# Keys and values by tokens in an mLSTM encoder: square blocks turned on VectorE and placed by four stores, instead of transposes on TensorE

## The chip, the cores and the metric

The kernel runs on one core of one Trainium2 chip. A core has TensorE (matrix products, "PE" in the profile, its weight loads "PEld"), VectorE ("DVE"), ScalarE ("ACT"), GpSimd ("POOL"), SyncE ("SP", which here only issues DMAs) and 16 DMA engines. The metric is device time in microseconds (us), the median of several runs.

## The reference, cut to what matters

One layer of a bidirectional encoder on 1280 tokens (1024 of a prompt, 256 of a sample) with 1024 channels. A normalised, modulated input `h` goes through one wide product `p = h @ w_in`; its columns are split into a convolution branch, gates, and the query, key and value of a matrix memory with 4 heads of 256 channels, worked out in chunks of 128 tokens and in both directions:

```python
h = rms_norm(x, norm_g) * (1.0 + scale) + shift
p = h @ w_in
cb, cc, cx, cz, q, k, v, o, mz, gpre, gmerge = split_combined(p)
...
# for each chunk of 128 tokens, qc, kc, vc: (batch, head, 128 tokens, 256 channels)
S = jnp.einsum('bhtd,bhsd->bhts', qc, kc) * Dexp
num = jnp.einsum('bhts,bhsd->bhtd', S, vc) + inter_w[..., None] * jnp.einsum('bhtd,bhde->bhte', qc, C)
...
C_new = decay[..., None, None] * C + jnp.einsum('bhs,bhsd,bhse->bhde', w, kc, vc)
```

The sum over `d` in the first line wants keys with channels on the partitions; the sums over tokens `s` in the second and the last want keys and values with tokens on the partitions. All of it is float32.

## The kernel before

The kernel has three stages. The first, which the change touches, makes all columns of `p`; the second (`Sweep`, `Pairs`) runs the matrix memory, with the convolution branch's projection as filler on TensorE; the third merges, projects and normalises.

**The products of the first stage.** Everything there lies with channels on the partitions and tokens along the free axis. Columns of `w_in` are taken in pairs of 128, tokens in two halves of 640 (`TH2`), the 1024 input channels in two halves: a 2 x 2 block product, done with seven products instead of eight (class `Strassen`). Each product is a job (function `go`): 24 pairs of a weight load and a matmul over 320 tokens (line 755), since each operand is split into a high and a low part and three of the four part products are taken. The weights of a job are prepared some steps ahead: DMA (line 318) into one of 3 `raw` tiles, sums of blocks on VectorE (`comb`, line 628), the high part on ScalarE (`wh`, line 329), the low part on GpSimd (`wl`, line 330). The result of a job stands in one of 3 PSUM tiles `acc`; VectorE adds it to an earlier part result (`plus`, line 672) into a tile `q` of 128 x 640, of which there are 5 (`new_q`, a ring used in the order of creation).

**The pairs of the heads.** For each of the 4 heads there is a pair for the keys, one for the values and one for the queries (`head_pairs`), those of head 0 about a sixth of the way into the span, those of heads 1 to 3 at the end of the first stage. Four of the seven jobs of a pair finish a result: 128 channels x 640 tokens, in jobs 2, 5, 6 and 7. A result of keys or queries is stored as it is (`kT_dr`, `qT_dr`, line 321). A result of keys or values goes through `by_tokens`, which turns it so that tokens are on the partitions, and stores it into `kn_dr` or `v_dr` (tokens x channels in DRAM), whence the second stage loads it. There are 4 heads x 2 x 4 = 32 such turns.

**One turn before.** TensorE transposes the five 128 x 128 blocks of the result (line 885) into two PSUM tiles `misc`, three and two blocks; ScalarE copies them (line 888) into a tile `q` called `vt`; one DMA stores `vt` with runs of 128 channels, 512 B each, 640 of them.

**The order.** Operations are recorded, not issued: `op(engine, cost, function, r=reads, w=writes)`. At the end of the first stage `board.play()` simulates all engines with the costs as written, and issues each engine's operations in the order in which that simulation began them. Each engine then works its list strictly in order, waiting on semaphores. A DMA is an operation of SP: 0.4 us to issue, then its size over a rate of 375 KB per us, then 2.2 us to land. In that simulation a turn of TensorE is given 1.0 us of slack (`slack=1.0`), so that it is put behind matmuls of the next job. While TensorE waits for the operand of one instruction, all that stands behind it in its list waits too; the same holds for VectorE and for SP.

`thirds`, which is also in the stretch of heads 1 to 3, makes part of the modulation on VectorE (line 1174) with two small matmuls (line 1181) at the end, also into `misc`. After the last pair, the first loads of the second stage are already in SP's list (`first_y`, into tiles `b00`, `b10`).

Of the kernel before, what the change touches and what calls it, by code (L numbers as in the profile page):

```python
# [16 lines left out]
P = 128  # L17
# [12 lines left out]
TH2 = T // 2  # L30
# [10 lines left out]
class Board:  # L41
# [25 lines left out]
    def buf(self, pool, shape, dt, tag, bufs, t=None):  # L67
        b = self.Buf(pool, shape, dt, tag, bufs, t)
        self.places.setdefault((id(pool), tag), []).append(b)
        return b  # L70

    def op(self, eng, us, f, r=(), w=(), after=(), low=False, slack=0.0):

        o = self.Op()
        o.eng, o.us, o.f, o.low, o.step, o.n, o.played, o.slack = eng, us, f, low, self.step, len(self.ops), False, slack
        o.before = set(after)
        for t in r:
            if t in self.writer:
                o.before.add(self.writer[t])
        for t in w:  # L80
            o.before.update(self.readers.get(t, ()))
            if t in self.writer:
                o.before.add(self.writer[t])
        for t in w:
            self.writer[t], self.readers[t] = o, []
        for t in r:
            if t not in w:
                self.readers.setdefault(t, []).append(o)
        o.before.discard(o)
        o.bufs = list(dict.fromkeys(b for t in (*r, *w) for b in (t if isinstance(t, tuple) else (t,)) if isinstance(b, self.Buf)))  # L90
        for b in o.bufs:
            b.users.append(o)
        self.ops.append(o)
        return o
# [87 lines left out]
def encoder_kernel(  # L182
# [7 lines left out]
    V, A, G, PE = nc.vector, nc.scalar, nc.gpsimd, nc.tensor  # L190
# [35 lines left out]
    ident = const.tile([P, P], F32, name="ident")  # L226
# [70 lines left out]
    op, buf = board.op, board.buf  # L297
# [22 lines left out]
    def store(kb, dst, src, r, w=()):  # L320
        op("SP", kb, lambda: dma(dst, src()), r=r, w=w)
# [236 lines left out]
    def qtile():  # L558
        return buf(rp, [P, TH2], F32, "q", 5)
# [5 lines left out]
    def misc_buf():  # L565
        return buf(psA, [P, 512], F32, "misc", 2)
# [19 lines left out]
    def whole(b):  # L586
        return Slice(b, slice(0, TH2))

    def new_q():
        return whole(qtile())  # L590
# [285 lines left out]


    def by_tokens(dst, t, r0, l):
        vt = new_q()
        for j0, jn in ((0, 3), (3, 2)):  # L880
            pv = misc_buf()

            def turn(j0=j0, jn=jn, pv=pv):
                for j in range(jn):
                    PE.transpose(pv[:, j * P:(j + 1) * P], t()[:, (j0 + j) * P:(j0 + j + 1) * P], ident[:])  # L885

            op("PE", .12 * jn, turn, r=[t.tok], w=[pv], slack=1.0)
            op("ACT", .2 + .1 * jn, lambda j0=j0, jn=jn, pv=pv: A.copy(vt()[:, j0 * P:(j0 + jn) * P], pv[:, :jn * P]),
               r=[pv], w=[(vt.b, j0)])
        store(320, dst[l * TH2:(l + 1) * TH2, r0:r0 + P].rearrange("(c p) d -> p c d", p=P),  # L890
              lambda: vt().rearrange("p (c d) -> p c d", d=P), [(vt.b, 0), (vt.b, 3)])

    def head_pair(col, dst, h):
        def result(b, l):
            r0 = h * HD + b * P

            def f(t):
                if col != CQ:
                    by_tokens(kn_dr if col == CK else v_dr, t, r0, l)
                if dst is not None:  # L900
                    store(320, dst[r0:r0 + P, l * TH2:(l + 1) * TH2], t, [t.tok])
            return None, f

        return Strassen(col + h * HD, col + h * HD + P, result(0, 0), result(1, 0), result(0, 1), result(1, 1))
# [716 lines left out]
    def second(s):  # L1621
        h, i = divmod(s - 10, 10)
        return (h, two_[h].order[i], i) if 0 <= h < NH else (None, None, None)
# [3 lines left out]
    for s in range(10 * NH + 15):  # L1627
# [4 lines left out]
        h, c, i = second(s - 3)  # L1632
        if h is not None and h + 2 < NH and c in (5, 7, 9):
            load_head(h + 2, (5, 7, 9).index(c))
        h, i = divmod(s, 10)
        mark = len(board.ops)
        if h < NH:
            c, d = one[h].order[i], one[h].d
# [8 lines left out]
        h, c, i = second(s)  # L1647
# [9 lines left out]
        h, c, i = second(s - 2)  # L1657
        if h is not None:
            prs[h, c - c % 2].values(c)
        h, c, i = second(s - 4)  # L1660
# [185 lines left out]
```

## Time and profile before

| | |
|---|---|
| median of 3 runs | 1730.31 us (1727.86 to 1730.43) |
| the profiled execution, its own time | 1726.71 us |
| span of the profiled execution | 1724.6 us |
| mean granted TensorE clock | 0.992 |
| busy: PE, PEld, DVE, ACT, POOL | 97%, 92%, 57%, 35%, 39% |
| chain that ended last: PE, DVE, issue | 91%, 5%, 2% |

The span runs from the first instruction to the last; the execution's own time is 2.1 us longer. Busy matmuls are pipelined, so a busy TensorE is not one at its peak; the time that a group of matmuls costs is read from the chain or from the starts of its neighbours. Where several engines are busy at once, only the one that the others wait for sets the time; the chain of waits tells which it was, and the table by stretches how much room the others have.

### The profile page before, as it was taken

The page shows a single profiled execution, that of the slowest core. Times are in us where ns is not written, and L with a number is a line of the kernel's source. Part 1 is how long each engine was busy: PE and PEld are TensorE (multiplying, and loading weights), DVE is VectorE, ACT ScalarE, POOL GpSimd, SP SyncE. Part 2 cuts the span into 40 slices and gives each one's busy share as a digit, 9 for nine tenths or more (in the row PEclk, how much of TensorE's full clock was granted, in tenths as well). Part 3 has the DMA queues.
Part 4 walks back from the last instruction along what each step waited for, and adds up shares of the span by engine and source line. Part 5 has one row for each costly group of instructions (what it writes and reads, how often), then busy time and mean ns, then how long its engine had stood idle before and what let it go on. Part 6 is the DMA issues. An engine that isn't in the chain of part 4 may idle for free.

```text
span 1724.6 us, 27940 instructions
## 1 busy us (share of the span) xinstructions
PE 1676.9 (97%) x10702; PEld 1591.3 (92%) x10702; DVE 974.6 (57%) x1657; ACT 604.4 (35%) x1185; POOL 679.5 (39%) x499
## 2 busy tenths in 40 slices
PE   7889999999999999999999999999999999999997
PEld 1789999899999999999999899999888889998986
DVE  1795433456555565566666765642247777565645
ACT  2753333224554222222222222222256565333322
POOL 1124333235665566667766533333210101323412
PEclk9899999999999999999999999999999999999999
DMA  9234323224553222222222434336878865684631
GB/s 332 87 109 146 115 91 121 64 74 122 148 155 108 57 68 68 80 80 63 65 61 89 141 108 138 117 117 231 284 232 273 269 199 162 219 282 135 229 112 61
DMA packets 217562, 241.88 MB, mean 140 GB/s; under 512 B 12645, under 2 KB 174677, under 8 KB 217429
## 3 DMA queue, kind: packets, MB, share of 16 engines
q1 hardware_dynamic: 217248, 240.06, 43.5%
q8 instruction: 85, 1.39, 0.3%
q14 instruction: 49, 0.39, 0.1%
q10 hardware_dynamic: 180, 0.04, 0.0%
HBM read 171.16 MB, written 68.89 MB: 139 GB/s over the span
## 4 chain that ended last, share of the span: by engine, by line
PE 91%; DVE 5%; issue 2%; ACT 1%; DMA 1%; ACTq 0%; SPq 0%; POOL 0%; DVEq 0%; POOLq 0%
PE acc L755 59%; PE u L1365 3%; PE qc L1347 3%; PE accd L1520 2%; PE accd L1521 2%; PE accd L1522 2%; PE accd L1733 2%; PE accd L1734 2%; PE accd L1732 2%; PE acc L1587 2%; PE acc L1588 2%; PE acc L1589 2%; PE acc L480 2%; PE misc L885 1%; PE misc L1408 1%
## 5 line engine op out<-in xcount | busy, mean ns | idle before, releaser
L672 DVE TENSOR_TENSOR q<-acc,q 128x640 f32<-128x640 f32 x272 | 220.6, 820 | 259.9 <-PE acc L755 249.5
L330 POOL TENSOR_TENSOR wl<-comb,wh 128x512 fp32r<-128x512 f32 x176 | 247.2, 1405 | 304.2 <-ACT wh L329 293.2
L330 POOL TENSOR_TENSOR wl<-raw,wh 128x512 fp32r<-128x512 f32 x136 | 191.6, 1409 | 250.9 <-ACT wh L329 245.1
L755 PE MATMUL acc<-xt,wh 128*128 128x320 f32 x1408 | 264.4, 310 | 0.0
L755 PEld LDWEIGHTS acc<-xt,wh 128*128 128x128 f32 x1408 | 220.6, 188 | 0.1
L329 ACT CAST wh<-comb 128x512 fp32r<-128x512 f32 x176 | 108.9, 619 | 243.6 <-PE acc L755 236.1
L329 ACT CAST wh<-raw 128x512 fp32r<-128x512 f32 x136 | 84.4, 621 | 286.5 <-PE acc L755 203.3
L755 PE MATMUL acc<-xt,wl 128*128 128x320 f32 x704 | 160.4, 309 | 0.0
L1548 POOL TENSOR_TENSOR wl<-raw,wh 128x512 fp32r<-128x512 f32 x28 | 36.3, 1300 | 233.7 <-ACT wh L1547 233.7
L755 PEld LDWEIGHTS acc<-xt,wl 128*128 128x128 f32 x704 | 117.7, 188 | 0.0
L628 DVE TENSOR_TENSOR comb<-raw 128x512 f32<-128x512 f32 x88 | 76.7, 872 | 46.7 <-DMA raw<-in_w_in_dram 31.2
L822 POOL TENSOR_TENSOR big<-big,q 128x640 f32<-128x640 f32 x48 | 78.8, 1641 | 37.1 <-DVE q L672 28.8
L572 ACT ACTIVATE q<-q,zero 128x640 f32<-128x640 f32 x76 | 63.2, 831 | 80.4 <-DVE q L672 74.8
L628 DVE TENSOR_TENSOR comb<-raw,comb 128x512 f32<-128x512 f32 x44 | 44.2, 1004 | 78.5 <-POOL wl L330 78.5
L755 PE MATMUL acc<-b00H,wh 128*128 128x320 f32 x352 | 83.0, 316 | 0.0
L755 PE MATMUL acc<-t2L,wh 128*128 128x320 f32 x352 | 80.3, 310 | 2.1 <-DVE t2L L384 2.1
L755 PE MATMUL acc<-b11H,wh 128*128 128x320 f32 x352 | 80.9, 310 | 1.5 <-ACT wh L329 1.5
L755 PE MATMUL acc<-t3H,wh 128*128 128x320 f32 x352 | 81.6, 313 | 0.0
L1520 PE MATMUL accd<-y,wh 128*128 128x320 f32 x256 | 79.9, 313 | 1.5 <-DVE og L1498 1.5
L755 PE MATMUL acc<-t2H,wh 128*128 128x320 f32 x352 | 80.8, 311 | 0.4 <-ACT t2H L383 0.4
L755 PE MATMUL acc<-b10H,wh 128*128 128x320 f32 x352 | 80.6, 309 | 0.4 <-DVE q L672 0.4
L755 PE MATMUL acc<-b11H,wl 128*128 128x320 f32 x352 | 80.1, 308 | 0.9 <-POOL wl L330 0.9
(320 smaller groups left out, 4195.4 us busy)
## 6 DMA issues: line engine op xcount, KB each, us to landing
raw<-in_w_in_dram SPq DMA_DIRECT2D x96, 256.0 KB
raw<-in_w_in_dram SPq DMA_DIRECT2D x46, 512.0 KB
th<-th_dr SPq DMA_DIRECT2D x32, 320.0 KB
th_dr<-q SPq DMA_DIRECT2D x28, 320.0 KB
raw<-in_w_proj_conv_dram SPq DMA_DIRECT2D x16, 512.0 KB
k<-kn_dr SPq DMA_DIRECT2D x64, 128.0 KB
raw<-in_w_proj_mlstm_dram SPq DMA_DIRECT2D x16, 512.0 KB
raw<-in_w_out_dram SPq DMA_DIRECT2D x16, 512.0 KB
```

Source lines behind the costliest of these rows:

```text
L329: op("ACT", .63, lambda: A.copy(wh[:], src()), r=r, w=[wh])
L330: op("POOL", 1.4, lambda: G.tensor_tensor(out=wl[:], in0=src(), in1=fp(wh[:]), op=ALU.subtract), r=[*r, wh], w=[wl])
L480: op("PE", .88, lambda h=h, j=j, kt=kt, wa=wa: PE.matmul(pada[h][0:4, j, :], cz4()[:, kt, :], wa()[:, j * 512:(j + 1) * 512], start=kt == ...
L572: A.activation(out, in_, AF.Tanh, bias=zero[:, 0:1], scale=0.5)
L628: op("DVE", .9, lambda: V.tensor_tensor(out=t[:], in0=x(), in1=y(), op=o), r=[x.tok, y.tok], w=[t])
L672: op("DVE", .82, lambda: V.tensor_tensor(out=two(dst()), in0=acc[:, :, 0:TQ], in1=two(t()), op=ALU.add), r=[acc, t.tok], w=[dst.tok])
L755: PE.matmul(acc[:, q, 0:TQ], st_[:, k_, :], m_[:, q * TQ:(q + 1) * TQ], start=k_ == 0 and n == 0, stop=k_ == 3 and n == 2)
L822: op("POOL", 1.65, lambda: G.tensor_tensor(out=dst(), in0=dst(), in1=t(), op=ALU.mult), r=[dst.tok, t.tok], w=[dst.tok])
L1347: PE.matmul(pq[:, 0:HD + 2], qTs[i][:, kd, c * P:(c + 1) * P], C[:, kd, :], start=kd == 0, stop=kd == 1)
L1365: PE.matmul(pu[:, db, 0:HD + 2], k[:, db * P:(db + 1) * P], wv[:], start=True, stop=True)
L1520: PE.matmul(accs[q][:, :TQ], wh, yH, start=kt == 0, stop=False)
L1548: op("POOL", 1.36, lambda wh=wh, wl=wl, src=src: G.tensor_tensor(out=wl[:], in0=src(), in1=fp(wh[:]), op=ALU.subtract), r=[raw, wh], w=[wl])
```

## The change

In `by_tokens` the transposes on TensorE, the two PSUM tiles and the copies on ScalarE are gone. One VectorE instruction turns the whole 128 x 640 tile in square blocks of 32 x 32, each in its place: `vt[32a+i, 32b+j] = t[32a+j, 32b+i]`. Now partition 32a+i holds, for each block b of 32 tokens, 32 channels of token 32b+i. The exchange of the blocks' places is left to the stores: for each of the four groups a of 32 partitions, one DMA of 80 KB writes runs of 32 channels (128 B), 32 x 20 = 640 of them, into the channel columns r0+32a to r0+32a+31 of the tokens. The bytes stored are the same 320 KB; the runs are a quarter as long and four times as many, and SP issues four DMAs where it issued one. In the simulation that makes the order, VectorE's turn costs 0.85 us.

```diff
     def by_tokens(dst, t, r0, l):
+
         vt = new_q()
-        for j0, jn in ((0, 3), (3, 2)):
-            pv = misc_buf()
-
-            def turn(j0=j0, jn=jn, pv=pv):
-                for j in range(jn):
-                    PE.transpose(pv[:, j * P:(j + 1) * P], t()[:, (j0 + j) * P:(j0 + j + 1) * P], ident[:])
-
-            op("PE", .12 * jn, turn, r=[t.tok], w=[pv], slack=1.0)
-            op("ACT", .2 + .1 * jn, lambda j0=j0, jn=jn, pv=pv: A.copy(vt()[:, j0 * P:(j0 + jn) * P], pv[:, :jn * P]),
-               r=[pv], w=[(vt.b, j0)])
-        store(320, dst[l * TH2:(l + 1) * TH2, r0:r0 + P].rearrange("(c p) d -> p c d", p=P),
-              lambda: vt().rearrange("p (c d) -> p c d", d=P), [(vt.b, 0), (vt.b, 3)])
+        op("DVE", .85, lambda: V.transpose(vt(), t()), r=[t.tok], w=[vt.tok])
+        for a in range(4):
+            cs = slice(r0 + 32 * a, r0 + 32 * a + 32)
+            store(80, dst[l * TH2:(l + 1) * TH2, cs].rearrange("(b i) j -> i b j", i=32),
+                  lambda a=a: vt()[32 * a:32 * a + 32].rearrange("p (b j) -> p b j", j=32), [vt.tok])
```

## Rows read from the trace of the kernel before

**Rows 1.** The page: busy time, share of the span, instructions of each engine.
```profile
PE 1676.9 (97%) x10702; PEld 1591.3 (92%) x10702; DVE 974.6 (57%) x1657; ACT 604.4 (35%) x1185; POOL 679.5 (39%) x499
```

**Rows 2.** Busy us by stretch, in engine order, then granted clock, DMA share, GB/s.
```profile
950.00:960.00 10.00, 10.00 (x70) 10.00 (x69) 10.00 (x14) 2.59 (x4) 6.19 (x5) 1.00 0.17 66
960.00:970.00 10.00, 6.52 (x38) 6.26 (x37) 7.15 (x6) 3.15 (x6) 8.30 (x6) 0.83 0.45 144
...
1038.20:1118.60 80.40, 80.40 (x552) 78.44 (x551) 45.13 (x85) 20.79 (x41) 28.11 (x24) 1.00 0.42 125
1118.60:1198.90 80.30, 79.34 (x547) 77.78 (x545) 28.99 (x46) 20.85 (x41) 27.97 (x23) 1.00 0.49 164
```

**Rows 3.** The chain, 255 to 345 and 940 to 1260 us: start, us, what.
```profile
289.24 0.55 PE misc L885 x5
...
963.68 2.01 DVE comb L628
965.69 0.75 DVE q L672
966.48 1.33 PE misc L885 x5
967.81 10.38 PE acc L755 x66
978.19 0.55 PE misc L885 x5
978.74 3.52 PE acc L755 x24
...
1174.52 0.55 PE misc L885 x5
1175.07 22.88 PE acc L755 x156
```

**Rows 4.** Order of time, 964 to 972 us, PE: start, us, instruction, idle before.
```profile
966.48 1.33 PE L885 MATMUL misc<-ident,q 128*128 128x128 f32 x5 [3.48 <-DVE q L672]
967.46 0.88 PE L755 MATMUL acc<-t3H,wh 128*128 128x320 f32 x2
...
971.87 0.31 PE L755 MATMUL acc<-xt,wh 128*128 128x320 f32 x1
```

**Rows 5.** Groups to 1199 us: busy us, mean ns of one, idle before.
```profile
L672 DVE TENSOR_TENSOR q<-acc,q 128x640 f32<-128x640 f32 x272 | 220.6, 820 | 259.9 <-PE acc L755 249.5 <-issue 7.2 <-DMA b10H<-yc_drH 2.7
L888 ACT COPY q<-misc 128x384 f32<-128x384 f32 x32 | 15.4, 481 | 66.0 <-PE misc L885 55.6 <-DMA kT_dr<-q 10.4
L888 ACT COPY q<-misc 128x256 f32<-128x256 f32 x32 | 12.1, 378 | 0.0
```

**Rows 6.** Order of time, 964 to 996 us, DVE.
```profile
963.68 2.01 DVE L628 TENSOR_TENSOR comb<-raw,comb 128x512 f32<-128x512 f32 x1
965.62 1.74 DVE L672 TENSOR_TENSOR q<-acc,q 128x640 f32<-128x640 f32 x2
972.07 0.82 DVE L672 TENSOR_TENSOR q<-acc,q 128x640 f32<-128x640 f32 x1 [4.72 <-PE acc L755]
...
985.84 0.67 DVE L628 TENSOR_TENSOR comb<-raw 128x512 f32<-128x512 f32 x1
```

**Rows 7.** Order of time, 960 to 972 us, POOL beside the slow VectorE sums.
```profile
963.17 1.98 POOL L866 TENSOR_TENSOR big<-big,q 128x640 fp32r<-128x640 f32 x1
965.11 1.71 POOL L330 TENSOR_TENSOR wl<-raw,wh 128x512 fp32r<-128x512 f32 x1
```

**Rows 8.** DMA packets, 155.5 to 157 us: packets, MB, share of 16 engines.
```profile
DMA packets 992, 0.06 MB, mean 42 GB/s; under 512 B 992, under 2 KB 992, under 8 KB 992
q1 hardware_dynamic: 992, 0.06, 44.5%
```

**Rows 9.** DMA packets, 298.4 to 303 us.
```profile
DMA packets 656, 0.33 MB, mean 71 GB/s; under 512 B 16, under 2 KB 656, under 8 KB 656
q1 hardware_dynamic: 656, 0.33, 26.7%
```

**Rows 10.** Order of time, 940 to 1190 us, SP: issues of DMAs.
```profile
1056.86 0.34 SPq L321 DMA_DIRECT2D kT_dr<-q  x1
1059.76 0.37 SPq L321 DMA_DIRECT2D kn_dr<-q  x1
1060.92 0.33 SPq L321 DMA_DIRECT2D kT_dr<-q  x1
...
1064.98 0.33 SPq L321 DMA_DIRECT2D kT_dr<-q  x1
...
1175.66 0.38 SPq L321 DMA_DIRECT2D v_dr<-q  x1
1176.85 0.93 SPq L318 DMA_DIRECT2D b00H<-yc_drH  x2
```

**Rows 11.** Waits 940 to 1199 us, TensorE's weight loads: us, times, longest.
```profile
PEld misc L1181 <- ACT q L888: 1.1, 6, 0.2
```

## Prediction

> **What bounds the kernel now.** I read the page first: TensorE is busy for 97% of the span, no other engine for more than 57% [rows 1]. That alone proves little, since it is a mean over stages, so the next view is the table by stretches. In the stretches of heads 1 to 3 TensorE is busy all of 80.4 us, VectorE 45, ScalarE 21, and the DMA engines have a share of 0.42 [rows 2]. The chain of waits says the same in order of time: from 978 us to 1198 us it is TensorE alone, matmuls of line 755 and, between them, the turns of line 885, each with 0.55 us [rows 3]. The reader is to see that a turn here stands on the path with its full length, with no wait before it and none behind: matmuls start the moment it ends. The turns of head 0, about 650 us earlier, stand in the chain with the same 0.55 us each [rows 3].
>
> One place differs. From 950 to 960 us, where the convolution ends and the heads begin, VectorE is busy 10.00 of 10 us, and from 960 to 970 TensorE is busy only 6.5, at a mean granted clock of 0.83 [rows 2]. The chain runs there through sums on VectorE and reaches TensorE by the first turn of head 1 [rows 3]: it waits 3.48 us for its operand, the result of the second job, and the whole list of TensorE stands behind it [rows 4]. So VectorE's lateness reaches TensorE through the very instruction that is removed.
>
> **What is removed from TensorE.** 32 turns. Of 31 I take 0.55 us each from the chain [rows 3]: 31 x 0.55 = 17.05 us. The one at 966.48 us is dearer. The job before it ended at 966.48 - 3.48 = 963.00 us; the next job (operand t3) began at 967.46 and took until 971.87, 4.41 us [rows 4], where 24 such matmuls take 3.52 elsewhere [rows 3]: its first ones ran at a lower granted clock after the wait. Without the turn that job can begin at about 963.0 and end at 966.5. The job after it needs a PSUM tile that the late sum frees: the pair of sums that begins at 965.62 ends its first about 0.8 us later, at 966.4 [rows 6], so it can begin at 966.5 in place of 971.87: 5.3 us. Of this I take 4.5, since the new turn on VectorE stands between these two sums and costs up to one instruction more (0.82 us) there. If the new order moves VectorE's work, it may be 0, or all 5.3. Sum: 17.05 + 4.5 = 21.5 us.
>
> **What is removed from ScalarE.** 64 copies, 15.4 + 12.1 = 27.5 us [rows 5]. ScalarE waits for TensorE there and is a quarter busy [rows 2]: worth nothing, but that `misc` is free at once. Six small matmuls of `thirds` waited 1.1 us in all for that copy [rows 11]; I leave it to the low end.
>
> **What is added to VectorE.** 32 turns of 128 x 640. The trace has no such instruction. The nearest rows: the sum of line 672, as many elements, 0.82 us [rows 5]; a sum of 512 elements between two SBUF tiles, 0.67 us when GpSimd rests and 2.01 when GpSimd works beside it [rows 6, 7]. From below I take 0.67, from above 2.01, and choose 0.82, as it has the same shape and reads one stream. What hides it is VectorE's room: in the 80.4 us of one head's three pairs it has 35 us idle, and 8 turns take 6.6 us, at the upper end 16. What is late if it stalls: the next sum of line 672 waits behind it, and with it the release of a PSUM tile; there are three, so TensorE notices only when VectorE is more than about one job (3.5 us) late. Price: 0. VectorE would bound these stretches only with 8 turns of (76 - 45.1)/8 = 3.9 us, where 76 is the new length, 80.4 - 8 x 0.55. The turn no longer waits behind matmuls, so the store can go out earlier: before, about 2.9 us lay between the issue of a result's own store and that of its turned form (1056.86 and 1059.76) [rows 10].
>
> The Trainium skill speaks against this step: "VectorE: DVE Perf Modes", section "Rules for kernel authors", gives a full 128 x 128 transpose to TensorE where PSUM will do, and keeps VectorE for blocks of 32. No run here shows its figure for VectorE, 311 ns for 128 columns of bf16; five of them would be an estimate of 1.6 us a turn, by which the sum would stay as it is.
>
> **What is added to SP.** A store takes SP 0.37 us [rows 10]; four take 1.48, so 32 x 1.11 = 35.5 us more in all. SP's list has gaps of microseconds between issues in these stretches [rows 10], so this is hidden, but for the last turn: behind its store stand the loads for the second stage, 1.2 us later [rows 10]. Up to 3 x 0.37 = 1.1 us are late there, and the transfers with them. I book 1.0 us.
>
> **What is added to the DMA engines.** A store of a turn had 640 runs of 512 B. The stretch that holds just one such store has 656 packets for 26.7% of 16 x 4.6 us, 19.65 us, or 30 ns each [rows 9]. It now has 2560 runs of 128 B. No row shows such a write. The nearest from below: a load in runs of 64 B, 992 packets for 44.5% of 16 x 1.5 us, 10.7 us, or 10.8 ns each [rows 8]. Between them in proportion to the bytes lies 10.8 + (64/448) x 19.2 = 13.5 ns, which I take; the bounds are 10.8 and 30. A turn's store then takes 2560 x 13.5 / 16 = 2.2 us of all engines, before 1.2; at 30 ns 4.8. Of one head's 80.4 us the DMA engines are busy 0.42 x 80.4 = 33.8, the 8 old stores 9.6 of them; 24.2 + 8 x 2.2 = 42 of 76 us is room enough. Price: 0.
>
> The Trainium skill, "DMA: Bandwidth & Descriptors", section "Why small descriptors are slow (HBM only)", adds about three cycles to the data beats of every packet; for 128 B that is 4 + 3 cycles, an estimate of 8 ns at the page's 850 MHz. The trace's two sizes lie above that rule's (30 ns where it gives 22). By it the stores would take 1.3 us a turn and the sum would be the same.
>
> **The sum.** 21.5 - 1.0 = 20.5 us less than the profiled execution's 1726.7 (a span of 1724.6 and 2.1 around it): 1706.2. The median of the runs shown lies 3.6 us above that execution; 1730.3 - 20.5 = 1709.8. I say 1709.
>
> **The rivals.** *The short runs cost as much as long ones* (30 ns). In a key pair three turns come at 4.06 us from each other (1056.86, 1060.92, 1064.98) [rows 10]. Three stores of 4.8 us and three of the keys themselves, of at most the 1.2 us of the same bytes in runs of 512 B, are 18 us of transfers in 12.2; the backlog of 6 us, and in a value pair (without the second store) of 14.4 - 12.2 = 2 us, holds tiles `q`, and VectorE, whose turn needs one at once, stands still with the sums behind it. If half of 4 x 6 + 4 x 2 = 32 us reaches TensorE (the three PSUM tiles hide some; half is my choice), that is 16: 1709.8 + 16 = 1726. For it: a write of 128 B stands in no row, and the stores share the queue with the weights. Against it: 64 B came at 10.8 ns [rows 8].
>
> *Slower: the short writes cost twice a long one* (60 ns), and DMA becomes the bound of the head pairs. 8 x 2560 x 60 / 16 = 76.8 us for a head, with 24.2 of other transfers 101 us, where it had 80.4: 20.6 x 4 = 82 us more, 1812. It decides from (80.4 - 24.2) / (8 x 160) = 44 ns on. Against it: one and a half times the price of 512 B would be needed.
>
> *VectorE's order* eats the gain: the planner places 32 more instructions on VectorE, and at 950 to 966 us it is already the bound [rows 2]. If the gain at 966 us is lost and another wait of as much arises in head 0 and at the hand-over to the second stage, 17 - 5 - 4 = 8 us remain: 1722. Were the turn over 3.9 us, the heads would be bound by VectorE and the change would lose.
>
> *No gain at all*, because TensorE then waits for weights in the same places: what speaks against it is that the chain shows no wait between 978 and 1198 us [rows 3], and that the weights' helpers sit idle for most of the time [rows 2].
>
> **How the numbers follow.** A gain of 15 to 25 us (1705 to 1715): 0.66. Partly eaten, by short runs at up to 30 ns or by VectorE's order (1715 to 1727): 0.16. Within 0.2% (3.5 us), about what a measurement of this kernel can tell from no change: 0.07. Slower: 0.11, of it 0.08 for writes above 44 ns and 0.03 for a turn above 3.9 us. So faster 0.82, same 0.07, slower 0.11. The range reaches down to 1702 (all 5.3 us, the 1.1 of `thirds`, no loss at the hand-over, and 4 us for runs as low as the profiled one) and up to 1727, through the second case.
>
> **What would show it.** Right: no line 885 or 888; the chain of the head stretches is line 755 alone; one head's three pairs take 76 us where they took 80.4; a VectorE group of 32 near 0.82 us; the wait of 3.48 us at the start of head 1 gone, and the clock of that stretch at 1.00; packets up by 32 x 1920 = 61,440 at 13 to 14 ns; 128 stores in place of 32. Wrong: stretches in which the DMA share nears 1 during keys and values; waits of VectorE's turn for stores; sums of line 672 held up behind turns; waits of `wh` or `comb` for weights that land late.

## The result and the profile after

| | before | after |
|---|---|---|
| median | 1729.09 us (1725.92 to 1730.43, 4 runs) | 1706.65 us (1704.44 to 1707.38, 4 runs) |
| profiled span | 1724.6 us | 1704.3 us |
| mean granted TensorE clock | 0.992 | 0.993 |

The ratio is 0.9873, with a 95% interval from 0.986 to 0.9887: 22.4 us, or 1.3%, faster. The forecast was 1709, with 1702 to 1727 around it.

The page after, busy time of each engine, answers to [rows 1]:

```profile
PE 1657.9 (97%) x10542; PEld 1571.2 (92%) x10542; DVE 996.0 (58%) x1689; ACT 579.4 (34%) x1121; POOL 677.9 (40%) x499
```

TensorE has 160 instructions and 19.0 us fewer, ScalarE 64 and 25.0 us fewer, VectorE 32 and 21 us more. TensorE's share of the span is still 97%: it stayed the bound and got less to do.

The chain after, in the stretch of the heads, answers to [rows 3]:

```profile
934.93 37.52 PE acc L755 x254
972.45 0.52 PE misc L1175 x2
972.97 24.84 PE acc L755 x168
997.81 0.52 PE misc L1175 x2
998.33 24.84 PE acc L755 x168
...
1124.61 0.52 PE misc L1175 x2
1125.13 24.84 PE acc L755 x168
```

Matmuls of line 755 alone, seven jobs (168 pairs) at a time; what still stands between them is the small product of `thirds`, 0.52 us. One head's three pairs now take 3 x (24.84 + 0.52) = 76.1 us, where they took 80.4.

The table by stretches, of the start of head 1 (answers to [rows 2]), and of a key, a value and a query pair; columns as there:

```profile
960.00:970.00 10.00, 10.00 (x68) 9.73 (x68) 8.41 (x9) 3.60 (x6) 8.87 (x8) 1.00 0.54 136
...
1034.00:1059.40 25.40, 25.40 (x173) 24.77 (x172) 17.84 (x33) 4.94 (x8) 9.33 (x8) 1.00 0.68 156
1059.40:1084.80 25.40, 25.40 (x172) 24.77 (x171) 17.84 (x33) 4.94 (x8) 9.33 (x8) 1.00 0.54 105
1084.80:1110.10 25.30, 25.30 (x172) 24.67 (x171) 14.74 (x29) 4.94 (x8) 9.32 (x8) 1.00 0.44 136
```

The stretch in which TensorE was busy for 6.5 us at a granted clock of 0.83 is now full, at 1.00. In the key and value pairs VectorE has 7.5 us of 25.4 idle. The DMA engines' share is not the same for the three: 0.68 with keys, 0.54 with values, 0.44 with queries. Nor is it the same for the heads. These rows are of head 2; the key pair of head 1, where loads of `thirds` and of weights come together, has 0.93, against 0.63 in the same stretch before:

```profile
964.50:989.90 25.40, 25.40 (x172) 24.67 (x171) 18.79 (x36) 4.94 (x8) 13.15 (x11) 1.00 0.93 213
```

TensorE is busy all the time there, so this costs the changed kernel nothing, but it is where the least room is left. The experiments come back to this.

The start of head 1 in order of time, VectorE and then TensorE, answers to [rows 4, 6]:

```profile
962.29 2.06 DVE L628 TENSOR_TENSOR comb<-raw,comb 128x512 f32<-128x512 f32 x1
964.28 0.81 DVE L672 TENSOR_TENSOR q<-acc,q 128x640 f32<-128x640 f32 x1
965.12 0.84 DVE L881 STREAM_TRANSPOSE q<-q 128x640 f32<-128x640 f32 x1
965.89 1.71 DVE L672 TENSOR_TENSOR q<-acc,q 128x640 f32<-128x640 f32 x2
```

```profile
961.53 0.56 PE L755 MATMUL acc<-t3H,wh 128*128 128x320 f32 x2
...
965.15 0.84 PE L755 MATMUL acc<-xt,wh 128*128 128x320 f32 x4
```

VectorE is as late as before: its sum of 2.06 us still ends just ahead of the late result. But nothing on TensorE waits for that result now. Job t3 ran from 961.53, and the job after it began at 965.15, the moment the sum at 964.28 had freed its PSUM tile.

The group of the new turn, and its issues on SP for the values (16 turns, 64 issues: shortest, median and longest ns):

```profile
L881 DVE STREAM_TRANSPOSE q<-q 128x640 f32<-128x640 f32 x32 | 27.0, 845 | 1.1
```

```profile
L321 SPq DMA_DIRECT2D v_dr<-q x64: 302/508/1986, 303.3 to 1158.2; - x64
```

A turn takes VectorE 845 ns. An issue takes SP 508 ns in the median and up to 1986, against 367 before.

DMA packets in 303.2 to 305.8 us, which hold little but the store of one turn, answer to [rows 9]:

```profile
DMA packets 1811, 0.23 MB, mean 88 GB/s; under 512 B 1811, under 2 KB 1811, under 8 KB 1811
...
q1 hardware_dynamic: 1811, 0.23, 58.4%
```

58.4% of 16 x 2.6 us for 1811 packets are 13.4 ns for a run of 128 B.

### The profile page after: what moved, and what is told of

It is laid out like the page before. It is cut to its first block, busy times and chain, and to the rows that moved or that the text cites. A ratio compares the mean times of both kernels' runs of the same rounds, so it can differ in the third digit from the quotient of the medians.

```text
span 1704.3 us, 27694 instructions
## 1 busy us (share of the span) xinstructions
PE 1657.9 (97%) x10542; PEld 1571.2 (92%) x10542; DVE 996.0 (58%) x1689; ACT 579.4 (34%) x1121; POOL 677.9 (40%) x499
## 4 chain that ended last, share of the span: by engine, by line
PE 91%; DVE 4%; issue 1%; DMA 1%; ACT 1%; ACTq 0%; SPq 0%; POOL 0%; DVEq 0%; POOLq 0%
PE acc L755 61%; PE qc L1341 3%; PE u L1359 3%; PE accd L1515 2%; PE accd L1514 2%; PE accd L1516 2%; PE accd L1727 2%; PE accd L1728 2%; PE accd L1726 2%; PE acc L1582 2%; PE acc L1581 2%; PE acc L1583 2%; PE acc L480 2%; PE misc L1402 1%; PE misc L1442 1%
## 5 line engine op out<-in xcount | busy, mean ns | idle before, releaser
L628 DVE TENSOR_TENSOR comb<-raw 128x512 f32<-128x512 f32 x88 | 72.8, 827 | 47.3 <-DMA raw<-in_w_in_dram 31.0
L755 PE MATMUL acc<-b11L,wh 128*128 128x320 f32 x352 | 80.6, 310 | 0.0
```

Of the source, the lines that this page charges most:

```text
L628: op("DVE", .9, lambda: V.tensor_tensor(out=t[:], in0=x(), in1=y(), op=o), r=[x.tok, y.tok], w=[t])
L755: PE.matmul(acc[:, q, 0:TQ], st_[:, k_, :], m_[:, q * TQ:(q + 1) * TQ], start=k_ == 0 and n == 0, stop=k_ == 3 and n == 2)
```

## The experiments

Two theories. The first, the prediction's: each turn stood on TensorE's path with 0.55 us, one of them also handed VectorE's lateness to TensorE with some 5 us, and what was added lies in idle time. The rival: turns are worth the same everywhere, the rest comes from the new order of all operations, and the short stores or VectorE's turns eat part of the gain.

**One turn alone, and all but that one.** Of the 32 turns only the one at the start of head 1 is made the new way, or only that one the old way:

```diff
-                    by_tokens(kn_dr if col == CK else v_dr, t, r0, l)
+                    (by_tokens if (col, h, b, l) == (CK, 1, 0, 0) else by_tokens_pe)(kn_dr if col == CK else v_dr, t, r0, l)
...
+                    (by_tokens if (col, h, b, l) != (CK, 1, 0, 0) else by_tokens_pe)(kn_dr if col == CK else v_dr, t, r0, l)
```

> Only one of the 32 turns is made the new way: the first result of the keys of head 1, for which TensorE had waited 3.48 us; the other 31 stay on TensorE. Theory (a turn costs TensorE 0.55 us, and this one also handed VectorE's lateness to TensorE's whole list): 5.3 us less than before, within 1.5. Rival (every turn is worth the same, about 0.7 us, and the rest of the gain comes from the new order of all operations): 0.7 us less, within 1. In the trace, the theory expects no wait of 3.5 us on TensorE between 940 and 1000 us.

> The other 31 turns are made the new way, that one stays on TensorE. Theory: 31 x 0.55 = 17 us less than before, the wait of about 3.5 us before that turn still there. Rival (all turns worth the same): 31/32 of the whole gain of 22.4, 21.7 us less.

One turn: 1722.27 us, 0.9958 of before (0.9946 to 0.9971), 7.1 us less. All but that one: 1712.37 us, 0.9901 (0.9886 to 0.9915), 17.0 us less. The rival's 0.7 lies outside the first interval (5.0 to 9.3 us less), its 21.7 outside the second (14.7 to 19.7). One turn of 32 gives a quarter to a third of the gain (5.4 us by the traces, below, and 7.1 by this run, of 22.4), the other 31 the 17 us of their time on TensorE. The 7.1 is more than the 5.3 within 1.5 that was expected; its interval holds 5.3. TensorE's first instruction of that kind with a wait, of the one and of the other:

```profile
978.75 0.74 PE L894 MATMUL misc<-ident,q 128*128 128x128 f32 x5 [1.35 <-DVE q L672]
```

```profile
963.03 0.76 PE L894 MATMUL misc<-ident,q 128*128 128x128 f32 x5 [3.48 <-DVE q L672]
```

With one turn changed, a part of the wait comes back: the next old turn, at 978.75, waits 1.35 us for VectorE. With 31 changed, the wait of 3.48 us stands where it was.

**The stores alone.** The turn on VectorE with one store in runs of 512 B (the exchange of the blocks' places is left out), and the old turn on TensorE with four stores in runs of 128 B:

```diff
-        for a in range(4):
-            cs = slice(r0 + 32 * a, r0 + 32 * a + 32)
-            store(80, dst[...].rearrange("(b i) j -> i b j", i=32), ...)
+        store(320, dst[l * TH2:(l + 1) * TH2, r0:r0 + P].rearrange("(c p) d -> p c d", p=P),
+              lambda: vt().rearrange("p (c d) -> p c d", d=P), [vt.tok])
```

```diff
-        store(320, dst[...].rearrange("(c p) d -> p c d", p=P), lambda: vt().rearrange("p (c d) -> p c d", d=P), ...)
+        for a in range(4):
+            cs = slice(r0 + 32 * a, r0 + 32 * a + 32)
+            store(80, dst[l * TH2:(l + 1) * TH2, cs].rearrange("(c p) j -> p c j", p=P),
+                  lambda a=a: vt().rearrange("p (c d) -> p c d", d=P)[:, :, 32 * a:32 * a + 32], [(vt.b, 0), (vt.b, 3)])
```

> The turn on VectorE as in the change, but one store of 320 KB with runs of 512 B as before; the exchange of the blocks' places is left out. Theory (the four stores with short runs lie in time that nothing waits for): the time of the changed kernel, within 2 us. Rival (the stores eat a part of the gain, through SP's 4 x 0.52 us or through a DMA share near 0.9 while keys are made): 4 us or more below the changed kernel.

> The turn on TensorE and ScalarE as before, but its result stored by four DMAs with runs of 128 B, as many packets as in the change. Theory: the time of the kernel before, within 2 us. Rival (the short stores cost): 4 us or more above it.

The first: 1705.90 us, 0.9862 of before (0.9849 to 0.9876), against the change's 0.9873: the same. The second: 1727.86 us, 0.9995 (0.9986 to 1.0004): the same as before. The four short stores cost nothing that shows, with the new turn or with the old.

**More work on VectorE.** The turn made twice or five times:

```diff
-        op("DVE", .85, lambda: V.transpose(vt(), t()), r=[t.tok], w=[vt.tok])
+        def turn():
+            for _ in range(2):      # or 5
+                V.transpose(vt(), t())
+
+        op("DVE", 1.70, turn, r=[t.tok], w=[vt.tok])      # or 4.25
```

> The changed kernel with each VectorE turn made twice over (1.7 us a turn in place of 0.85, also in the simulation that makes the order). Theory (VectorE's turns lie in idle time): the time of the changed kernel, 1706.6 us, within 2.5. Rival (VectorE is already close to the bound while keys and values are made): 27 us more work on VectorE, of which a third or more shows, 9 us or more.

> Each VectorE turn made five times (4.2 us a turn), above the 3.9 us from which, by the prediction, VectorE would bound the stretches of the heads. Theory: slower than the changed kernel by 10 to 45 us (VectorE has 45 + 8 x 4.2 = 79 us of work for a head whose TensorE work is 76, and three turns come in a row, one for each job of 3.5 us). Rival (VectorE has more room than that sum gives it): within 3 us of the changed kernel.

Twice: 1706.77 us, 0.9869 (0.9855 to 0.9884): nothing. Five times: 1735.26 us, 1.0039 (1.0022 to 1.0055): 28.6 us above the change and slower than before. In its table by stretches VectorE is then the busy one and TensorE waits:

```profile
950.00:1040.00 90.00, 77.73 (x495) 74.00 (x494) 86.95 (x134) 16.24 (x27) 35.76 (x29) 0.94 0.49 123
```

So a turn may cost VectorE 1.7 us without loss, and at 4.2 us the whole gain is gone; the prediction's 3.9 us lies between. That does not confirm the 3.9, which is a mean over a head's three pairs, of which only two have turns. In a key or value pair VectorE does 17.84 us, 3.4 of them turns; the other 14.5 leave (25.4 - 14.5)/4 = 2.7 us for each of four turns, and no run lies between 1.7 and 4.2. The largest of TensorE's waits from 250 to 1290 us is again an instruction in its list whose operand VectorE makes late, the small product of `thirds`:

```profile
PE misc L1179 <- DVE big L1172: 13.4, 3, 7.3
```

**More transfers.** One more store of 320 KB for each turn, into a DRAM tile that nothing reads, in runs of 64 B, 32 B and 128 B:

```diff
+        x_dr = dram.tile([P, TH2 // 16, 32], F32, name=...)      # 16: runs of 64 B; 8: 32 B; 32: 128 B
+        store(320, x_dr[:, :, 0:16], lambda: vt().rearrange("p (n j) -> p n j", j=16), [vt.tok])
```

> The changed kernel with one store more per turn: the turned tile once more, 320 KB in 5120 runs of 64 B, into a DRAM tile that nothing reads. At 10.8 ns each these are 3.5 us of all DMA engines, so a turn costs 5.7 us in place of 2.2, as if a run of 128 B cost 35 ns. If the mean room decides (24 + 8 x 5.7 = 70 of 76 us for a head): within 3 us of the changed kernel. If the bunching of three turns decides, as in the rival on short runs: 15 to 30 us more.

> The same with runs of 32 B, 10240 of them, some 6.4 us at 10 ns: a turn costs 8.6 us, as if a run of 128 B cost 54 ns. By the mean room 24 + 8 x 8.6 = 93 us for a head of 76: 17 us more for each of four heads, 68 us more than the changed kernel, and slower than the kernel before. If the DMA engines do not bound even then: within 3 us of the changed kernel.

> The changed kernel with one store more per turn, 320 KB in 2560 runs of 128 B into a DRAM tile that nothing reads: a turn costs the DMA engines 4.4 us, as if a run of 128 B cost 27.5 ns, which is the prediction's first rival. By its rule (half of the backlog of three turns in a row reaches TensorE): some 12 us more than the changed kernel, about 1719. If the mean room decided: within 3 us. If the cost grows as steeply as with runs of 64 B (37 us for 3.5 us more a turn): 20 us or more.

64 B: 1743.92 us, 1.0085 (1.0066 to 1.0104), 37 us above the change. 32 B: 1832.57 us, 1.0594 (1.0575 to 1.0613), 126 above. 128 B: 1711.87 us, 0.9907 (0.9892 to 0.9922), 5 above. None of the three came out as expected: 37 where the dearer theory had 15 to 30, 126 where it had 68, and 5 where the choices were 3 at most, some 12, or 20 and more. The mean room of a head did not decide. With runs of 64 B it should have been enough, by some 10 us a head (34 us free, 8 stores of 3.0), and the gain was not only lost but turned into a loss; the prediction's 44 ns, from which the short writes would make the change lose, was too high, as 32 ns for each run of a turn (13.4 and two of 9.4) did it. The DMA packets of the 64 B kernel in 316 to 318 us, nearly all of them in runs of 64 B (0.17 MB), give the price of such a write, 80.1% of 16 x 2 us for 2713 packets, 9.4 ns:

```profile
DMA packets 2713, 0.17 MB, mean 87 GB/s; under 512 B 2713, under 2 KB 2713, under 8 KB 2713
...
q1 hardware_dynamic: 2713, 0.17, 80.1%
```

What a backlog of transfers does is seen in head 0 of that kernel, SP and then VectorE in order of time:

```profile
289.49 0.34 SPq L321 DMA_DIRECT2D kT_dr<-q  x1
...
300.05 4.17 SPq L321 DMA_DIRECT2D kT_dr<-q  x1
```

```profile
306.52 0.84 DVE L881 STREAM_TRANSPOSE q<-q 128x640 f32<-128x640 f32 x1 [2.98 <-DMA x_drFalse<-q]
...
322.82 0.69 DVE L628 TENSOR_TENSOR comb<-raw 128x512 f32<-128x512 f32 x1 [10.95 <-DMA raw<-in_w_in_dram]
```

The same issue of a key store that took SP 0.34 us takes 4.17 behind the stores of two more turns, and all behind it in SP's list is late, the weights among it: a sum of weight blocks waits 10.95 us for its load (3.48 in the changed kernel). A turn waits 2.98 us for a tile that a store still reads. That much the first rival had told. But none of it reaches TensorE in head 0. It is busy equally long in the changed kernel (first line) and in this one:

```profile
250.00:345.00 95.00, 92.70 (x627) 89.11 (x625) 42.06 (x72) 20.44 (x33) 30.30 (x24) 0.98 0.41 97
```

```profile
250.00:345.00 95.00, 92.70 (x637) 89.83 (x636) 41.97 (x73) 21.57 (x34) 30.71 (x24) 1.00 0.62 114
```

Where the time is lost is told by the small product of `thirds`, which stands once in each of eight pairs, from the keys of head 1 to the values of head 3. Against the changed kernel it is late by 0.6, 6.4, 13.6, 13.9, 19.8, 25.9, 25.9 and 25.9 us. So heads 1 and 2 cost 25.3 us, the keys and values of head 3 nothing. The first product of the matrix memory is 36.2 us late, so the hand-over to the second stage costs 10 more; the span ends 40.0 us later. In heads 1 and 2 TensorE waits 17.3 us, in eight pieces; seven of them, 14.0 us, are for sums on VectorE:

```profile
PE acc L755 <- DVE q L672: 14.0, 7, 3.6
```

The rest goes for the greater part with a lower granted clock behind these waits (0.72 in 996 to 1002 us). One of the seven, VectorE and then TensorE:

```profile
1086.54 0.35 DVE L1170 SCALAR_TENSOR_TENSOR big<-big,cols 128x128 f32<-128x128 f32 x1 [4.74 <-DMA big<-in_w_ada_dram]
...
1087.44 0.82 DVE L672 TENSOR_TENSOR q<-acc,q 128x640 f32<-128x640 f32 x1
```

```profile
1088.40 0.82 PE L755 MATMUL acc<-xt,wh 128*128 128x320 f32 x4 [3.59 <-DVE q L672]
```

VectorE waits for a load of `thirds`, which stands in SP's list behind the stores; the sum behind it in VectorE's list is late, and TensorE waits for that sum. With runs of 128 B the loss inside the heads is at one such place alone, behind the keys of head 1, the pair with the least room:

```profile
1000.54 0.87 PE L755 MATMUL acc<-b11H,wh 128*128 128x320 f32 x2 [2.52 <-DVE q L672]
```

The last load of `thirds` that VectorE needs there was issued at 994.58 us, in the changed kernel at 985.49. The seven jobs behind the wait take 27.66 us on the chain in place of 24.84, at a granted clock of 0.61 in 1002 to 1008 us: 2.5 + 2.8 = 5.3 us, and no other pair up to the values of head 3 loses anything.

For runs of 32 B, 286 to 288 us hold 3424 packets for 82.3% of the engines, 7.7 ns each:

```profile
DMA packets 3424, 0.11 MB, mean 55 GB/s; under 512 B 3424, under 2 KB 3424, under 8 KB 3424
...
q1 hardware_dynamic: 3424, 0.11, 82.3%
```

Can the loss be summed from the room of single pairs? In head 2 of the changed kernel the DMA engines work 0.68 x 25.4 = 17.3 us in a key pair, 13.7 in a value pair. Four more stores each take 4 x 3.0 us (64 B), 4 x 2.1 (128 B) or 4 x 4.9 (32 B). What goes beyond 25.4, taken for four heads alike, is 17, 2 and 79 us, where 37, 5 and 126 were measured. The sum has the order right and tells that each loses, but it is too low for all three, and the traces do not bear it out: the heads do not lose alike (with 32 B the small product of head 1's keys is already 20.5 us late, with 64 B 0.6), and with 64 B a quarter of the loss is at the hand-over. How the waits of VectorE, SP and the DMA engines add up, above all to the 126 us, stays open.

**More issues, hardly more bytes.** Four stores more per turn, of 4 KB each:

```diff
+        x_dr = dram.tile([P, 32], F32, name=...)
+        for a in range(4):
+            store(4, x_dr[32 * a:32 * a + 32], lambda a=a: vt()[32 * a:32 * a + 32, 0:32], [vt.tok])
```

> The changed kernel with four stores more per turn, each of only 32 runs of 128 B (4 KB): SP issues 8 DMAs a turn in place of 4, the DMA engines have 5% more to do. If it is the transfer time that made the extra stores dear: within 3 us of the changed kernel. If it is SP's issues: 10 us or more above it.

1708.91 us, 0.9898 (0.9875 to 0.992), 2.3 us above the change: within the 3 us expected of the theory that it is the transfers, though its four runs reach from 1707.44 to 1714.42. With this, SP issues 8 stores a turn; that the extra stores of 64 B cost 37 us is not due to the number of issues. The issues are not free, though. Behind the keys of head 1 the chain runs through SP's issues of turned stores from 993 to 998 us, then through a load of `thirds` and VectorE, and TensorE waits at the same place as with runs of 128 B:

```profile
1002.90 0.53 PE L755 MATMUL acc<-b00H,wh 128*128 128x320 f32 x2 [2.18 <-DVE q L672]
```

## Why the prediction was right, point by point

- **31 turns at 0.55 us, 17.05 us: right.** All but one turn gave 17.0 us.
- **The turn at the start of head 1, 5.3 us or, as I took it, 4.5: right in its mechanism, 0.9 low in the sum.** Before, the job after t3 began at 971.87 [rows 4]; after, at 965.15. The key result of head 1 is stored at 966.45 before and at 965.12 after, 1.3 us earlier by what had been gained until then, so 6.7 - 1.3 = 5.4 us were gained on the spot. The allowance of 0.8 us for the turn between VectorE's two sums was not needed.
- **ScalarE's copies and the small matmuls: worth nothing that can be told**, as said.
- **VectorE's turn at 0.82 us, hidden: right.** 0.845 us, and twice that costs nothing either. The Trainium skill, "VectorE: DVE Perf Modes", section "The three transpose paths", has 311 ns for 128 columns of bf16, a type that no turn here has. The estimate of 1.6 us a turn from it was too high: 640 columns of float32 took 845 ns, 169 ns for 128, and the measurement decides.
- **SP's issues: mis-sized, and without effect.** Four issues took 4 x 0.51 = 2.0 us, not 1.48. The 1.0 us booked for the hand-over to the second stage is not found: that stage begins at 1179.80 in place of 1198.90, in both kernels 0.95 us after the last matmul of line 755, and its first product of the matrix memory follows 8.6 us later, before 9.1.
- **A run of 128 B at 13.5 ns: right, 13.4, with some luck.** The lower of the two rows it was taken between was a load; a write of 64 B takes 9.4 ns, not 10.8, and the same proportion from there gives 12.3. The rule of the Trainium skill, "DMA: Bandwidth & Descriptors", section "Why small descriptors are slow (HBM only)", from which I had estimated 8 ns, gives too little for this write.
- **The room of the DMA engines: wrong by its measure.** I compared a mean over the three pairs of one head, 42 of 76 us. In head 2 it is 17.3 of 25.4 with keys, in head 1 0.93 of the time. A sign that I had named for being wrong, a share near 1 during keys, is there in the changed kernel, and the loads behind it were still early enough, so the forecast stood. But the threshold of 44 ns was worked out from the mean, and with transfers of 32 ns a run the kernel lost. The first rival had the mechanism (a turn that waits for a store's tile, with the sums behind it late) but not its size: by its rule 27.5 ns a run cost some 12 us, and 5 were measured.
- **VectorE's 3.9 us: the same measure, not tested.** By pairs the bound is 2.7 us; the runs leave everything between 1.7 and 4.2 open.
- **The sum.** 17.05 + 5.4 = 22.45 us, against 22.4 between the medians: what the forecast of 20.5 lacked are the 0.9 at head 1 and the 1.0 booked for the hand-over. That the sum meets the medians so closely may be partly luck. In the two profiled executions 20.5 us were gained between the first key store of head 0 and the start of the second stage, which is 22.45 less 1.5 for a lower clock (below), 20.9; the whole spans differ by 20.3. The profiled execution before was 2.4 us quicker than its median; no run tells why.

## What to carry to other kernels

Where the chain shows one engine without a gap, work taken from it comes back in full, at the duration that it has in the chain; and an instruction in that engine's list that waits for another engine costs its wait too, so moving the one instruction that waits can be worth ten others. Room on the engines that take the work over must be read in the fullest stretch in which they take it, not from a mean and not from one head taken for all: here the DMA engines' share was 0.42 in the mean of head 2 before, 0.68 in its key pair after and 0.93 in that of head 1, and the smallest excess was paid there first. Short DMA runs are cheap until transfers lag; then the issuing queue stands still, and what is behind in it is late. Whether that costs anything depends on who waits for what is late: with runs of 64 B nobody on the path did in head 0, while in heads 1 and 2 it was VectorE, and behind it TensorE.

## What the runs showed of the hardware that was not expected

- TensorE waits 2.30 us for the gates' operand in both kernels (lines 939 and 933). Before, its granted clock stayed at 1.00 (2.4 GHz); after, it fell toward the lower level (1.2 GHz) behind the wait, 0.90 in the mean of 312 to 326 us, and two matmuls took 0.73 us in place of 0.46. The 64 matmuls there took 11.05 us on the chain in place of 9.51, 1.5 us of the gain. The kernel with one changed turn, whose head 0 is that of before, waits 2.30 us too and has the lower clock (0.88 in 312 to 326 us); the kernel with extra runs of 64 B, whose head 0 is changed, waits 2.30 us and stays at 1.00. So the change alone does not decide it, and no run tells what does. The changed kernel in the slow stretch and behind it, where 16 matmuls take the 2.50 us that they took before:

```profile
312.63 0.73 PE L933 MATMUL acc<-b00H,q 128*32 128x320 f32 x2
...
317.11 2.50 PE L933 MATMUL acc<-xt,q 128*32 128x320 f32 x16
```

- Issues on SP grow long where many short transfers are under way: no store of keys or values by tokens took more than 0.39 us to issue before, up to 2.2 with the change; a key store took 0.34 us at rest and up to 4.17 with stores of 64 B ahead of it, when the DMA engines' share had been 0.89 for 5 us.
- Writes in short runs cost 7.7 ns (32 B), 9.4 (64 B) and 13.4 (128 B) a packet, against 30 for 512 B [rows 9]: by the byte dearer, by the run cheaper, without a step between these four sizes.
